# Three GpSimd subtractions and one more split weight pair at the start of the expert stage

## The chip, the cores and the metric

The kernel runs on one core of one Trainium2 chip. The metric is the time of one execution in device microseconds; before the change the median of three runs is 1587.92 us (1586.55 to 1590.53). Matrix products run on PE (TensorE), elementwise work on DVE (VectorE), ACT (ScalarE) and POOL (GpSimd), and SP issues most of the DMAs.

## The reference

One layer of an encoder on 1024 tokens of width 1024: an input projection, three mixers side by side (retention, S5, windowed attention), an output projection, a LayerNorm, then an expert-choice SwiGLU and a last LayerNorm. The change lies in the experts:

```python
def expert_choice_ffn(x, router_w, w_gate, w_up, w_down):
    cap = EC_FACTOR * seq // N_EXPERTS                       # 128 tokens for each of 16 experts
    aff = jax.nn.softmax(jnp.einsum('bld,de->ble', x, router_w), axis=-1)
    gates, idx = lax.top_k(jnp.swapaxes(aff, 1, 2), cap)
    xs = x[bidx, idx]
    hdn = jax.nn.silu(jnp.einsum('becd,edf->becf', xs, w_gate)) * jnp.einsum('becd,edf->becf', xs, w_up)
    out = jnp.einsum('becf,efd->becd', hdn, w_down) * gates[..., None]
    return jnp.zeros_like(x).at[bidx, idx].add(out)
```

All of it is in float32, with 2048 hidden columns for each expert.

## The kernel before, in words

**Pieces.** The weights of the 16 experts come as 384 pieces of 128 x 2048 float32 (1 MB each), numbered in the order of their use (`order`, built in `Experts.__init__`). A quarter of an expert takes four pieces for the gate and up products and, one quarter late, two pieces of the down product. So pieces 0 to 3 are the first quarter's gate and up, 4 to 7 the second's, 8 and 9 the first quarter's down, 10 to 13 the third's gate and up, 14 and 15 the second's down.

**Split or whole.** A split piece is brought to the form of two numbers: `high` (L2288) makes ACT round it to fp32r, `low` (L2297) makes DVE subtract that from the raw piece, and `mm3_piece` (L2228) does 12 matmuls of 512 columns: first four with the high parts of both sides, then four with the tokens' low parts, then four with the weights' low parts. Only the last four need the result of `low`. The pairs in `WHOLE` (pieces 0 and 1, 4 and 5, 10 and 11) are not split: `load_whole` (L2278) brings two pieces into one buffer, and `mm_whole` (L2236) does 4 matmuls in float32 on tokens that are float32 as well. They need neither ACT nor DVE.

**Order.** The order on each engine is written out by hand. After piece t, `quarter` issues `high` for piece t + 4 and `low` for piece t + 3. `low` of a piece also issues the load (L2271) of the piece that stands five places further in the list of split pieces, into the buffers of `wraw`, of which there are five; such a load waits until the buffer's last reader is done, and SP issues its DMAs strictly in order.

**The top-k beside it.** The first expert's tokens are known early (from a ranking of expert 0 alone). The top-k of all experts (`top_k`) runs while the first expert's pieces are worked on, one step after each piece, on DVE and PE: eight rounds of maxima (L2111, L2114), then a bitonic merge (`bitonic`, L1866 and L1867: maximum and minimum of two halves of one SBUF tile), with the copies L2124 and the maxima L2126 between its three parts, at last the reversed copy `rev` (L2130). Two transposes on PE (L2133, L2134) stand behind it, then `mm` on DVE (L2136, L2137), a transpose (L2140), `tau` and `taus` on DVE (L2142, L2144), a transpose (L2147), the flags `g` (L2150) and the counting matmuls (L2155 to L2161), from which come the slots, the one-hot tiles (L2174) and the gather of the second expert's tokens by GpSimd (L2190).

Of the kernel before, what the change touches and what calls it, by code (L numbers as in the profile page):

```python
# [9 lines left out]
F32 = mybir.dt.float32  # L10
# [5 lines left out]
OP = mybir.AluOpType  # L16
# [28 lines left out]
def level(pool, n):  # L45

    pool.tile([P, n // 4], F32, name="level")
# [26 lines left out]
def constants(K, I):  # L74
    nc, cp = K.nc, K.consts
    K.ident = cp.tile([P, P], F32, name="ident")
    make_identity(nc, K.ident)
    K.mhalf = cp.tile([P, 4], F32, name="mhalf")
    nc.gpsimd.memset(K.mhalf, -0.5)
# [23 lines left out]
class Units:  # L103
# [9 lines left out]
    def high(self, i):  # L113
        u = self.K.hl[self.side].tile([P, 2, 1024], F32R, name="whl", tag="whl", bufs=2)
        self.K.nc.scalar.activation(u[:, 0, :], self.raw[:, i, :], AF.Copy)
        self.u[i] = u[:, 0, :], u[:, 1, :]

    def low(self, i):
        hi, lo = self.u[i]
        self.K.nc.vector.tensor_tensor(lo, self.raw[:, i, :], hi.bitcast(F32), OP.subtract)  # L120
# [1659 lines left out]
def attention_steps(K, F, zero, out, qs, mat, spaces):  # L1780
# [26 lines left out]
    for c in range(NT):  # L1807
# [21 lines left out]
        for j in range(2):  # L1829
            for low, kind in enumerate(("YS", "YT")):  # L1830
                at(c, kind, j, fn=lambda c=c, j=j, low=low: out_proj_split(K, c, j, low))
# [40 lines left out]
def top_k_consts(K):  # L1872

    nc, cp = K.nc, K.consts
    K.order01 = cp.tile([P, 2, P], BF16, name="order01")
    nc.gpsimd.memset(K.order01, 1.0)
    nc.gpsimd.affine_select(K.order01[:, 0, :], K.order01[:, 0, :], pattern=[[1, P]], base=-1, channel_multiplier=-1,
                            compare_op=OP.is_ge, fill=0.0)
    K.slots = cp.tile([P, P], F32, name="slots")
    nc.gpsimd.iota(K.slots, pattern=[[1, P]], base=-L, channel_multiplier=0, allow_small_or_imprecise_dtypes=True)  # L1880
    K.aff = cp.tile([P, NT, E], F32, name="aff")
    K.tok = cp.tile([P, NT, E, 5], BF16, name="tok")
    nc.gpsimd.iota(K.tok[:, :, :, 0], pattern=[[P, NT], [0, E]], base=0, channel_multiplier=0,
                   allow_small_or_imprecise_dtypes=True)
    nc.gpsimd.iota(K.tok[:, :, :, 1], pattern=[[0, NT], [0, E]], base=0, channel_multiplier=1,
                   allow_small_or_imprecise_dtypes=True)
    K.slot = cp.tile([P, NT, E], F32, name="slot")
# [351 lines left out]
class Experts:  # L2239
# [4 lines left out]


    RING = 6
    WHOLE = 0, 4, 10
    sort = None

    def __init__(self, K, I, O):  # L2250
        self.K, self.I, self.O = K, I, O
        self.order = []
        for q in range(4 * E + 1):
# [3 lines left out]
            if q:  # L2257
                e, f = divmod(q - 1, 4)
                self.order += [I["exp_w_down"][e, f, half] for half in range(2)]
        self.whole = [k + i for k in self.WHOLE for i in range(2)]  # L2260
        self.parted = [k for k in range(len(self.order)) if k not in self.whole]
# [18 lines left out]
    def high(self, k):  # L2280

        while self.highs <= min(k, len(self.order) - 1):
            k1, self.highs = self.highs, self.highs + 1
            if k1 in self.whole:
                continue
            pool, tag = (self.K.hy, "hy") if k1 in (6, 7) or k1 >= 12 and k1 % 6 not in (1, 3) else (self.K.hla, "whl")
            u = self.whl[k1] = pool.tile([P, 2, 2048], F32R, name="whl", tag=tag)
            self.K.nc.scalar.activation(u[:, 0, :], self.raw[k1].rearrange("p a b -> p (a b)"), AF.Copy)  # L2288

    def low(self, k):  # L2290

        while self.lows <= min(k, len(self.order) - 1):
            k1, self.lows = self.lows, self.lows + 1
            if k1 in self.whole:
                continue
            u, raw = self.whl[k1], self.raw.pop(k1).rearrange("p a b -> p (a b)")
            self.K.nc.vector.tensor_tensor(u[:, 1, :], raw, u[:, 0, :].bitcast(F32), OP.subtract)  # L2297
            i = self.parted.index(k1)
            if i > 1:
                self.load(i + 5)  # L2300
# [259 lines left out]
def build(tc, nc, I, O):  # L2560
    K = Ctx()
    K.tc, K.nc = tc, nc
    K.unit = 0

    def pool(name, side="left", **kw):
        cm = tc.tile_pool(name=name, bufs=kw.pop("bufs", 1), **({} if "space" in kw else {"side": side}), **kw)
        return cm, cm.__enter__()

    def close(*cms):
        for cm in cms:  # L2570
            cm.__exit__(None, None, None)

    _, dr = pool("scratch", space=DRAM)
    K.h_dram = [dr.tile([P, D], F32, name=f"h_d{t}") for t in range(NT)]
    K.y_dram = [dr.tile([P, 2, P], F32, name=f"y_d{t}") for t in range(NT)]
    K.q_dram = [[dr.tile([P, 4, 4, P], F32, name=f"q_d{h}_{k}") for k in range(2)] for h in range(2)]
    K.h1_dram = dr.tile([L, D], F32, name="h1_d")
    K.acc_dram = dr.tile([L, D], F32, name="acc_d")
    K.bx_dram = [[dr.tile([P, 8, 16], F32, name=f"bx_d{d}{g}") for g in range(2)] for d in range(2)]
    K.wo_dram = [[dr.tile([P, 8, 144], F32, name=f"wo_d{d}{g}") for g in range(2)] for d in range(2)]  # L2580
    K.s_dram = [[dr.tile([P, 8, P], F32, name=f"s_d{d}{g}") for g in range(2)] for d in range(2)]
    K.m_dram = [dr.tile([P, 8, P], F32, name=f"m_d{g}") for g in range(2)]
    K.kv_dram = [dr.tile([P, 2, 256], F32, name=f"kv_d{t}") for t in range(NT)]
    K.u_dram = dr.tile([P, 2, 8, P], F32, name="u_d")

    c_ps, K.pmm = pool("pmm", space=PSUM, bufs=2)
    c_pt, K.ptp = pool("ptp", space=PSUM, bufs=2)
    c_pa, K.pat = pool("pat", space=PSUM, bufs=2)
    c_po, K.po = pool("po", space=PSUM, bufs=1)
    c_sm, K.psm = pool("psm", space=PSUM, bufs=1)  # L2590

    c_con, K.consts = pool("consts")
    constants(K, I)
    K.gates = K.consts.tile([P, E], F32, name="gates")
    K.index = K.consts.tile([P, E], U32, name="index")
    top_k_consts(K)
    level(K.consts, 224)
    c_raw, K.raw = pool("raw", bufs=2)
    c_hy, K.hy = pool("hy", bufs=4)
    c_edge, edge = pool("edge", side="right")  # L2600
    level(edge, 224)
    hl = [pool(f"hl{i}", bufs=2, side="right") for i in range(2)]
    K.hl = [x[1] for x in hl]
    c_hl0, K.c_hl1 = (x[0] for x in hl)
    _, K.s5small = c_s5s = pool("s5small")
    c_s5s = c_s5s[0]
    K.c_ret, K.ret = pool("ret", side="right")
    K.S = K.ret.tile([P, NT, 256], F32, name="S")
    nc.gpsimd.memset(K.S[0:64, 0, :], 0.0)
    nc.gpsimd.memset(K.S[64:P, NT - 1, :], 0.0)  # L2610
    K.QT = K.ret.tile([P, 2, L], F32, name="QT")
    K.hT = [], []
    for half in range(2):
        for s in range(2):
            K.hT[s].append(K.hy.tile([P, KC, L // 2], F32R, name=f"hT{s}", tag="hy"))
    K.P, K.Y, K.at = {}, {}, {}
    T = mybir.EngineType
    hold = tc.manual_schedule(engines={T.PE, T.Activation, T.DVE, T.Pool, T.SP})
    hold.__enter__()
    K.mr, K.st, K.pr, K.ps, K.pt, K.pT, K.av, K.rpt, K.soft, K.ah, K.rank = ({} for _ in range(11))  # L2620
    X = K.X = Experts(K, I, O)
    K.next_raw = lambda k: (K.raw if k < 4 or (k - 4) % 5 > 2 else K.raw2).tile([P, 2, 1024], F32, name="wraw")
    K.psums, K.c_hl0 = (c_sm, c_po, c_pa, c_pt, c_ps), c_hl0
    c_ast, c_early, c_opy, c_op, c_tk, c_hla, c_xt = front(K, I, pool, close)
    close(c_tk, c_op, c_opy, c_early, c_ast, c_s5s)
    c_ex, K.ex = pool("ex")
    level(K.ex, 192)
    c_raw2, K.raw2 = pool("raw2", bufs=3)
    c_sel, K.sel = pool("sel")
    for half in range(2):  # L2630
        X.tokens(0, half, X.xF[:, half * 4:half * 4 + 4, :])
    for i in range(4, 6):
        X.load(i)
    expert_gather(K, 0, K.numbers)
    X.load(6)
    X.load_whole(10)
    X.sort = top_k(K)
    raw0 = []

    def sorted_out():  # L2640
        close(c_sel)
        raw0.append(pool("raw0", bufs=3))
        K.raw0 = raw0[0][1]
    K.sorted = sorted_out
    for q in range(4 * E + 1):
        X.quarter(q)
    last_rows(X, E - 1)
    assert not X.before and not X.after and not X.sort
    hold.__exit__(None, None, None)
    close(raw0[0][0], c_raw2, c_ex, c_hy, c_raw, c_con, c_xt, c_hla, c_edge, *K.psums)  # L2650
# [60 lines left out]
```

## Time and profile before

| what | value |
|---|---|
| median of three runs | 1587.92 us |
| the profiled execution | 1588.15 us |
| its span | 1586.4 us |
| granted TensorE clock | 0.993 |
| PE, DVE, ACT, POOL busy | 98%, 88%, 70%, 12% |
| subtractions L2297 on DVE | 378, 2285 ns each (median) |
| whole matmuls L2236 | 24, recorded as 48 |

In the profile's rows a group reads `line engine op out<-in shapes xcount`, with busy time and mean, and in brackets the idle time before it and what ended that. A float32 matmul of a whole piece is recorded as two entries, so a whole piece is `x8` and a split piece `x12`. Times in a timeline are microseconds from the start of the span. `SPq` rows are DMA issues.

### The profile page before, as it was taken

The numbers are of one execution on the slowest core, as the hardware profiler recorded it, in microseconds if no ns is written. First come the engines' busy times: TensorE is split into PE (matmuls) and PEld (weight loads), VectorE is DVE, ScalarE is ACT, GpSimd is POOL, SyncE is SP. The second block draws the span as 40 slices with busy tenths as digits, with TensorE's granted clock in tenths as the row PEclk, the third lists the DMA queues.
The fourth block names the chain that finished last, engine by engine and source line by source line (L and its number), as shares of the span: only waits on it lengthen the run. The fifth ranks groups of instructions, "written<-read, shape, count | busy, mean of one in ns | idle before, by whom it ended". The sixth has DMA issues, their size and how long they took to land.

```text
span 1586.4 us, 21018 instructions
## 1 busy us (share of the span) xinstructions
PE 1553.3 (98%) x7673; PEld 1277.0 (80%) x7673; DVE 1402.3 (88%) x1725; ACT 1118.2 (70%) x1281; POOL 191.9 (12%) x244
## 2 busy tenths in 40 slices
PE   7999999999989999999999999999999999999997
PEld 5887888788866788888888888888888888888886
DVE  7986974888887989999899998989999999999996
ACT  4645464877735677777777777777877878787783
POOL 4001211111110101010100101000201102020121
PEclk9999999999999999999999999999999999999999
DMA  5555569334258999999999999999999999999993
GB/s 183 207 153 128 148 195 283 103 95 147 102 195 347 357 387 403 383 389 395 371 385 384 372 385 377 398 410 418 405 413 414 405 414 415 410 413 415 408 421 145
DMA packets 101242, 506.78 MB, mean 319 GB/s; under 512 B 12817, under 2 KB 25873, under 8 KB 50450
## 3 DMA queue, kind: packets, MB, share of 16 engines
q1 hardware_dynamic: 84834, 474.50, 76.9%
q0 software_dynamic: 16304, 30.94, 6.9%
q8 instruction: 60, 0.98, 0.2%
q14 instruction: 44, 0.36, 0.1%
HBM read 461.36 MB, written 42.99 MB: 318 GB/s over the span
## 4 chain that ended last, share of the span: by engine, by line
PE 64%; DVE 14%; DMA 12%; issue 4%; ACT 4%; POOL 1%; SPq 0%; POOLq 0%; DVEq 0%; ACTq 0%
PE gu L2228 27%; PE y L2228 14%; DVE whl L2297 7%; DMA wraw<-in_exp_w_down 6%; PE mm L64 4%; PE mm L66 4%; PE mm L65 4%; DMA wraw<-in_exp_w_up 3%; PE tp L2211 2%; ACT whl L2288 1%; PE po L1458 1%; PE tp L1438 1%; PE at L1387 1%; DVE hT L56 1%; PE gu L2236 1%
## 5 line engine op out<-in xcount | busy, mean ns | idle before, releaser
L2297 DVE TENSOR_TENSOR whl<-wraw,whl 128x2048 fp32r<-128x2048 f32 x378 | 857.6, 2287 | 65.3 <-ACT whl L2288 62.9
L2288 ACT ACTIVATE whl<-wraw 128x2048 fp32r<-128x2048 f32 x378 | 724.2, 1919 | 244.7 <-PE gu L2228 69.1
L2228 PE MATMUL gu<-whl,xT 128*128 128x512 f32 x3000 | 712.3, 394 | 0.0
L2228 PEld LDWEIGHTS gu<-whl,xT 128*128 128x128 f32 x3000 | 555.4, 188 | 114.6 <-issue 1.0
L2228 PE MATMUL y<-whl,hT 128*128 128x512 f32 x1536 | 359.5, 389 | 0.0
L2228 PEld LDWEIGHTS y<-whl,hT 128*128 128x128 f32 x1536 | 288.0, 188 | 59.7
L2190 POOL DMA_INDIRECT xs<-h_d,index x15 | 29.9, 1992 | 456.5 <-PE y L2228 301.4
L64 PE MATMUL mm<-hT,whl 128*128 128x512 f32 x160 | 65.4, 409 | 0.0
L55 ACT ACTIVATE hT<-tp 128x512 fp32r<-128x512 f32 x80 | 46.0, 583 | 25.7 <-PE tp L163 14.3
L65 PE MATMUL mm<-hT,whl 128*128 128x512 f32 x160 | 62.5, 391 | 0.0
L66 PE MATMUL mm<-hT,whl 128*128 128x512 f32 x160 | 62.5, 391 | 0.0
L56 DVE TENSOR_TENSOR hT<-tp,hT 128x512 fp32r<-128x512 f32 x80 | 54.1, 683 | 4.2 <-ACT hT L55 4.1
L64 PE MATMUL mm<-WO,yh 128*128 128x512 f32 x128 | 53.4, 417 | 0.0
L66 PE MATMUL mm<-WO,yl 128*128 128x512 f32 x128 | 50.7, 396 | 0.0
L65 PE MATMUL mm<-WO,yh 128*128 128x512 f32 x128 | 50.5, 395 | 0.0
L64 PE MATMUL mm<-whl,hT 128*128 128x512 f32 (+1 forms) x128 | 47.2, 369 | 0.0
L2338 DVE TENSOR_TENSOR hid<-hid,gu 128x512 f32<-128x512 f32 x64 | 43.5, 680 | 3.8 <-PE gu L2228 3.8
L66 PE MATMUL mm<-whl,hT 128*128 128x512 f32 (+1 forms) x128 | 44.5, 347 | 1.5 <-DVE hT L56 1.5
L65 PE MATMUL mm<-whl,hT 128*128 128x512 f32 (+1 forms) x128 | 44.5, 348 | 0.1
L2332 ACT ACTIVATE hid<-gu 128x512 f32<-128x512 f32 x64 | 37.2, 581 | 8.4 <-PE gu L2236 8.4
L2211 PEld LDWEIGHTS tp<-ident,hid 128*128 128x128 f32 x256 | 31.3, 140 | 11.4 <-DVE hid L2338 3.7
L1398 DVE CUSTOM_DVE_ANT_0 S<-at,R,sink 128x384 f32<-128x384 f32 (+1 forms) x64 | 36.8, 577 | 3.9 <-PE at L1387 3.3
(429 smaller groups left out, 1778.0 us busy)
## 6 DMA issues: line engine op xcount, KB each, us to landing
wraw<-in_exp_w_up SPq DMA_DIRECT2D x128, 1024.0 KB, 8.1
wraw<-in_exp_w_down SPq DMA_DIRECT2D x128, 1024.0 KB, 8.6
wraw<-in_exp_w_gate SPq DMA_DIRECT2D x122, 1024.0 KB, 7.9
wraw<-in_w_in SPq DMA_DIRECT2D x8, 1024.0 KB, 7.5
whole<-in_exp_w_gate SPq DMA_DIRECT2D x6, 1024.0 KB, 10.2
x<-in_x SPq DMA_DIRECT2D x8, 512.0 KB, 4.5
h_d<-x SPq DMA_DIRECT2D x8, 512.0 KB, 3.2
q_d<-kst SPq DMA_DIRECT2D x32, 128.0 KB, 2.8
```

The lines of the kernel that those rows point to most:

```text
L55: nc.scalar.activation(hi, src, AF.Copy)
L56: eng.tensor_tensor(lo, src, hi.bitcast(F32), OP.subtract)
L64: nc.tensor.matmul(ps, a[0], b[0], start=start, stop=False)
L65: nc.tensor.matmul(ps, a[0], b[1], start=False, stop=False)
L66: nc.tensor.matmul(ps, a[1], b[0], start=False, stop=stop)
L1398: K.nc.vector.tensor_tensor_reduce(S[g][:, :W], K.at.pop((i, g))[:, :W], K.R[:, ro:ro + W], 2.0 ** -(h + 1), K.sink[:, h:h + 1], OP.add, O ...
L2211: K.nc.tensor.transpose(pt[:, c, :], src[:, (c0 + c) * P:(c0 + c + 1) * P], K.ident)
L2228: nc.tensor.matmul(ps, a[s][c], u[:, t, i * w:(i + 1) * w], start=first and id(ps) not in began, stop=last and left[id(ps)] == 0)
L2288: self.K.nc.scalar.activation(u[:, 0, :], self.raw[k1].rearrange("p a b -> p (a b)"), AF.Copy)
L2297: self.K.nc.vector.tensor_tensor(u[:, 1, :], raw, u[:, 0, :].bitcast(F32), OP.subtract)
L2332: nc.scalar.activation(self.h[q], self.pg[q][0], AF.Silu)
L2338: at(self.after, q, 3, lambda: nc.vector.tensor_tensor(self.h[q], self.h[q], self.pg[q][1], OP.mult))
```

## The change

`WHOLE` loses pieces 10 and 11. They are now split like the others: they come by `load` into `wraw`, ACT makes their high parts, and PE does 12 matmuls for each. `ASIDE` names pieces 7, 10 and 13: their subtraction is issued on GpSimd. Piece 11's subtraction is on DVE. The high parts and low parts of 10 and 11 lie in two buffers of the pool `hy`, where the whole pair had one. Pieces 7 and 13 leave DVE, piece 11 is new there.

```diff
-    WHOLE = 0, 4, 10
+    WHOLE = 0, 4
+    ASIDE = 7, 10, 13
...
-            pool, tag = (self.K.hy, "hy") if k1 in (6, 7) or k1 >= 12 and k1 % 6 not in (1, 3) else (self.K.hla, "whl")
+            pool, tag = (self.K.hy, "hy") if k1 in (6, 7, 10, 11) or k1 >= 12 and k1 % 6 not in (1, 3) else (self.K.hla, "whl")
...
-            self.K.nc.vector.tensor_tensor(u[:, 1, :], raw, u[:, 0, :].bitcast(F32), OP.subtract)
+            e = self.K.nc.gpsimd if k1 in self.ASIDE else self.K.nc.vector
+            e.tensor_tensor(u[:, 1, :], raw, u[:, 0, :].bitcast(F32), OP.subtract)
...
     X.load(6)
-    X.load_whole(10)
     X.sort = top_k(K)
```

In the changed kernel the lines stand one or two further down (L2288 becomes L2289, L2297 becomes L2299). On DVE, in the middle of the bitonic merge, before the change (`o64` and `m64` end the first part of the merge, `whl_5369` is piece 7, `hT1_5408` the low part of the first hidden quarter):

```order
L2124 COPY o64_5389<-b_5386 64x128
L2126 TENSOR_TENSOR m64_5391<-b_5386,o64_5389 64x128
L2297 TENSOR_TENSOR whl_5369<-wraw_5229,whl_5369 128x2048
L56 TENSOR_TENSOR hT1_5408<-tp_5398,hT0_5407 128x512
L1866 TENSOR_TENSOR b_5411<-m64_5391 64x64
```

and after it:

```order
L2124 COPY o64_5386<-b_5383 64x128
L2126 TENSOR_TENSOR m64_5388<-b_5383,o64_5386 64x128
L56 TENSOR_TENSOR hT1_5405<-tp_5395,hT0_5404 128x512
L1866 TENSOR_TENSOR b_5408<-m64_5388 64x64
L1867 TENSOR_TENSOR b_5408<-m64_5388 64x64
```

Piece 7's subtraction has left this place. At the end of the merge, on DVE before the change (`whl_5506` is piece 12, `whl_5526` piece 13, `whl_5552` piece 14):

```order
L2130 COPY rev_5504<-b_5501 32x128
L2136 COPY mm_5523<-tp_5520 128x16
L2137 TENSOR_TENSOR mm_5523<-mm_5523,tp_5520 128x16
L2297 TENSOR_TENSOR whl_5506<-wraw_5271,whl_5506 128x2048
L56 TENSOR_TENSOR hT1_5543<-tp_5533,hT0_5542 128x512
L2142 TENSOR_REDUCE tau_5548<-tp_5546 16x1
L2144 COPY taus_5550<-tau_5548 16x128
L2297 TENSOR_TENSOR whl_5526<-wraw_5372,whl_5526 128x2048
L2150 TENSOR_TENSOR g_5563<-aff_134,tp_5561 128x128 x2
```

and after it (`whl_5482` is piece 11, `whl_5510` piece 12, `whl_5567` piece 14):

```order
L2130 COPY rev_5508<-b_5505 32x128
L2299 TENSOR_TENSOR whl_5482<-wraw_5369,whl_5482 128x2048
L2136 COPY mm_5530<-tp_5527 128x16
L2137 TENSOR_TENSOR mm_5530<-mm_5530,tp_5527 128x16
L2299 TENSOR_TENSOR whl_5510<-wraw_5393,whl_5510 128x2048
L56 TENSOR_TENSOR hT1_5558<-tp_5540,hT0_5557 128x512
L2142 TENSOR_REDUCE tau_5563<-tp_5561 16x1
L2144 COPY taus_5565<-tau_5563 16x128
L2150 TENSOR_TENSOR g_5586<-aff_134,tp_5584 128x128 x2
```

Piece 11's subtraction stands between `rev` and `mm`, and piece 13's between `taus` and `g` is gone. On GpSimd, after the change (the rows ahead are the last steps of the top-k's preparation, `xs_5701` the gather of the second expert's tokens; `whl_5366`, `whl_5452` and `whl_5533` are pieces 7, 10 and 13):

```order
L1897 TENSOR_TENSOR rest1_5200<-rest0_5199,tok_135 128x16
L1895 CAST tok_135<-rest1_5200 128x16
L2299 TENSOR_TENSOR whl_5366<-wraw_5229,whl_5366 128x2048
L2299 TENSOR_TENSOR whl_5452<-wraw_5271,whl_5452 128x2048
L2299 TENSOR_TENSOR whl_5533<-wraw_5423,whl_5533 128x2048
L2190 DMA xs_5701<-h1_d_77,index_128 128x1024
```

The three stand in a row, between the preparation and the gather; before, nothing stood there.

## The prediction

> **What bounds the kernel now.** I read the page first, then the busy time by stages, then the chain that ended last around the first expert.
>
> ```profile
> span 1586.4 us, 21018 instructions
> core 0: us, PE busy (x) PEld busy (x) DVE busy (x) ACT busy (x) POOL busy (x), PEclk, DMA share, GB/s
> 481.00:500.60 19.60, 18.24 (x69) 12.11 (x68) 18.75 (x54) 10.43 (x7) 0.00 (x0) 1.00 0.99 409
> 500.60:523.00 22.40, 22.40 (x106) 15.35 (x107) 18.92 (x25) 13.36 (x10) 0.00 (x0) 1.00 0.69 240
> 560.00:1560.00 1000.00, 998.34 (x4642) 822.01 (x4641) 933.14 (x615) 776.18 (x570) 111.98 (x72) 1.00 1.00 399
> ```
>
> From 560 us on PE is busy 998 of 1000 us: what arrives late there stays late to the end. In the first expert (481 to 500.6) it is DVE that is full, 18.75 of 19.60 us, and PE is not. GpSimd does nothing. The chain says what DVE's work there decides:
>
> ```profile
> 483.27 2.20 DVE whl L2297
> 485.78 0.24 DVE b L1866
> 486.59 0.23 DVE o L2124
> 487.05 2.27 DVE whl L2297
> 489.33 0.60 DVE hT L56
> 491.36 2.20 DVE whl L2297
> 495.10 2.27 DVE whl L2297
> 500.20 0.21 DVE b L1866
> 500.60 0.24 PE tp L2133
> 500.85 0.25 PE tp L2134
> 501.10 0.59 PE tp L2211 x4
> 501.68 3.44 PE gu L2236 x8
> 505.23 3.44 PE gu L2236 x8
> 508.66 0.17 PE tp L2147
> ```
>
> From 483 to 500.6 us it runs through DVE alone: the subtractions of pieces 6, 7, 8 and 9 (four rows of L2297), and the steps of the merge between them, one after another. Then PE takes over: transposes, pieces 10 and 11, the next transpose. So each microsecond on DVE ahead of 500.6 counts, until PE no longer waits:
>
> ```profile
> 493.63 5.60 PE L2228 MATMUL y<-whl,hT 128*128 128x512 f32 x24
> 500.60 0.24 PE L2133 MATMUL tp<-ident,b 32*128 32x32 f32 x1 [1.36 <-DVE b L1867]
> 521.53 11.18 PE L2228 MATMUL gu<-whl,xT 128*128 128x512 f32 x48
> 500.58 0.21 DVE L2130 COPY rev<-b 32x128 f32<-32x128 f32 x1
> 501.34 0.17 DVE L2137 TENSOR_TENSOR mm<-mm,tp 128x16 f32<-128x16 f32 x1
> 505.72 2.27 DVE L2297 TENSOR_TENSOR whl<-wraw,whl 128x2048 fp32r<-128x2048 f32 x1
> ```
>
> PE waits 1.36 us for the merge; `rev` ends at 500.79.
>
> **The split pair on PE.** Four split pieces in a row take 11.18 us, a pair 5.59. The whole pair takes 3.44 + 3.44 = 6.88. Between the same transposes PE saves 6.88 - 5.59 = **1.29 us**, all on the path.
>
> **DVE's own work.** Piece 7's subtraction leaves the path ahead of `rev`: **-2.27 us**. Piece 13's (505.72, 2.27 us) stood beside PE's matmuls of piece 11: nothing. Piece 11's is new between `rev` and `mm`. Its cover is piece 10 on PE: that begins 501.68 - 500.79 = 0.9 us after `rev` and ends 0.9 + 2.8 = 3.7 us after it; 2.28 us of subtraction and some 0.4 us of `mm` are done by 2.7. Nothing, with 1.0 us to spare; a further hold of DVE there is paid beyond that 1.0.
>
> **GpSimd's three subtractions.** No row has one of this size. The nearest on the same engine:
>
> ```profile
> L257 POOL TENSOR_TENSOR rsmall<-rsmall 128x8 f32<-128x8 f32 x1 | 0.2, 205 | 0.1
> L261 POOL TENSOR_TENSOR w<-lg,col 128x4 f32<-128x4 f32 x2 | 0.4, 203 | 0.1
> L1897 POOL TENSOR_TENSOR rest<-aff,tok 128x16 f32<-128x16 f32 x8 | 1.8, 223 | 0.7
> ```
>
> From 4 to 16 columns it grows by 20 ns, 1.67 ns a column; from 8 to 16 by 18 ns, 2.25 a column. For 2048 columns that gives 0.2 + 3.4 = 3.6 us or 0.2 + 4.6 = 4.8 us. I take the middle, 4.2; the lower bound is DVE's 2.28 for the same shape.
>
> PE can wait that long. Piece 7's low part is needed for its last four matmuls only, and here is when ACT has the high parts:
>
> ```profile
> 481.32 1.91 ACT L2288 ACTIVATE whl<-wraw 128x2048 fp32r<-128x2048 f32 x1 [3.35 <-DMA wraw<-in_exp_w_up]
> 488.36 0.60 ACT L2332 ACTIVATE hid<-gu 128x512 f32<-128x512 f32 x1 [0.17 <-PE gu L2236]
> 488.86 1.91 ACT L2288 ACTIVATE whl<-wraw 128x2048 fp32r<-128x2048 f32 x1
> 496.60 1.92 ACT L2288 ACTIVATE whl<-wraw 128x2048 fp32r<-128x2048 f32 x1 [5.84 <-PE y L2228]
> ```
>
> Piece 7's ends at 483.23, so GpSimd can begin while DVE is on piece 6; piece 10's now stands at 488.86 and ends at 490.8. ACT's two new roundings fit into the 5.84 us in which it waited.
>
> What matters is whether the two engines can run side by side:
>
> ```profile
> 1255.28 4.49 DVE L2297 TENSOR_TENSOR whl<-wraw,whl 128x2048 fp32r<-128x2048 f32 x2
> 1258.33 1.48 POOL L2466 TENSOR_SCALAR fst<-fst 128x1 f32<-128x1 f32 x1 [4.49 <-ACT yl L2465]
> 446.86 2.30 DVE L2297 TENSOR_TENSOR whl<-wraw,whl 128x2048 fp32r<-128x2048 f32 x1
> 446.73 0.29 POOL L1897 TENSOR_TENSOR rest<-rest,tok 128x16 f32<-128x16 f32 x1
> 447.08 2.17 POOL L1895 CAST tok<-rest 128x16 bf16<-128x16 f32 x1
> L2297 DVE TENSOR_TENSOR whl<-wraw,whl x378: 2271/2285/2301, 446.9 to 1564.5; 128x2048 fp32r<-128x2048 f32 x189
> ```
>
> A one-column GpSimd step at 1258.33 takes 1.48 us and ends at 1259.81, with DVE's subtraction (1259.77). A 16-column cast that falls into a subtraction takes 2.17 us and ends at 449.25; the subtraction ended at 449.16. So GpSimd stands still while DVE subtracts two SBUF tiles. The other direction shows faintly: the one subtraction at whose start a GpSimd step was already running (446.73) is the longest of all 378, 2301 ns against 2285. I take it that whoever starts first holds the other for its whole run. The Trainium skill says so too ("SBUF — State Buffer", "Who interferes with whom"): DVE with two SBUF inputs and GpSimd reading SBUF exclude each other, and issue order decides; the trace agrees for DVE ahead of GpSimd and has no long case of the reverse. This rule speaks against the change.
>
> All merge steps L1866 and L1867 have two SBUF inputs, like the subtractions, and DVE works in order: one blocked step blocks the rest. Piece 7 on GpSimd starts behind piece 6's subtraction on DVE, at about 485.5, and holds the merge **4.2 us**, to 489.7. PE needs the result for the last third of piece 7, 2.8/3 = 0.9 us before it goes on to piece 8 at 493.63: 3 us to spare. Piece 10 is ready at 490.8, still inside the merge: **4.2 us** more. Now `rev` ends at 500.79 - 2.27 + 8.4 = 506.9.
>
> Piece 13's load waits for piece 8's subtraction on DVE (end of the third L2297 row, 493.56, now 493.56 - 2.27 + 8.4 = 499.7).
>
> ```profile
> DMA to landing us min/median/max: 4.7/7.8/18.6
> ```
>
> With DMA at 0.69 of its time here I take 4.7: landed at 504.4, rounded by ACT at 506.3. So GpSimd starts it at the last steps of the merge or at piece 11's subtraction right behind `rev`: **4.2 us** again, in the first case in full, in the second less the 1.0 to spare. With the median 7.8 it falls later, under PE's work on piece 11, and costs about 1.
>
> Nothing else is on the path. Piece 12's load waits on SP for GpSimd's piece 7, with 13 and 14 queued behind it; two pieces fewer lie ready in advance, but piece 12 lands by 489.7 + 4.7 = 494.4 and is needed past 508.66; without that cover PE would wait what is missing. The gather behind the three on GpSimd needs slots that depend on PE's work after piece 13: no delay of its own.
>
> Sum: -1.29 - 2.27 + 3 x 4.2 = **+9.0 us**. The 1.36 us that PE waits is at the same place, so none of the delay is absorbed. The profiled execution took 1588.15, of which 1586.4 is its span; 1597.2 there, and 0.2 less against the median of 1587.92: **1597 us**. With 3.6 and 4.8 for a hold it is +7.2 and +10.8: 1595 to 1599. The Trainium skill gives a size for GpSimd's step ("GPSIMD Engine Reference", 3.1): 4497 ns against DVE's 2293 for a tensor_tensor of 2048 float32; DVE's row agrees (2285), no row has the other, and by it the estimate would be +9.9.
>
> **The rivals.**
>
> *No hold in this direction.* GpSimd's reads slip in between DVE's. Then DVE is 2.27 us earlier at `rev`, PE's wait of 1.36 goes (what is late next is PE itself), and the split pair saves 1.29: -2.65, 1585.3 us. For it: no DVE step in the trace is seen waiting for microseconds on GpSimd. Against it: the clear wait in the other direction, and the 2301. It decides if the merge step behind piece 6's subtraction starts within 0.2 us.
>
> *Smaller holds.* If GpSimd is as fast as DVE, three holds of 2.28 give 6.84 - 3.56 = +3.3, 1591.2. If piece 13's falls under cover, 8.4 + 1 - 3.56 = +5.8, 1593.7.
>
> *More than the holds.* Holds of 4.8 and a PE wait on piece 13, which lands late (7.8 instead of 4.7, another 3.1): +13.9, 1601.8.
>
> **How the numbers follow.** Three full holds 0.50, smaller 0.20, none 0.22, more 0.08. A measurement of this kernel tells about 0.3%, 4.8 us, from no change: 1583.2 to 1592.7 is the same. Faster by more has no mechanism here, 0.03; the same takes the rest of no hold and half of the smaller ones, 0.29; slower 0.68. The range reaches from no hold (1585) to near the end of the last case (1601); the likeliest case has 1595 to 1599.
>
> **What would show it.** Right: three L2299 rows on POOL of about 4.2 us or more, the DVE step behind piece 6's subtraction starting some 4 us later, and PE's wait at L2133 grown from 1.36 to over 7 us, less what PE then waits at pieces 8 and 9. Pieces 10 and 11 take 5.6 us on PE. Wrong: DVE's steps keep their spacing beside GpSimd's rows, or PE's wait at L2133 is gone.

## The result, and the profile after

The changed kernel takes 1602.16 us (median of 6 runs, 1599.68 to 1605.08), the kernel before, run beside it, 1590.73 (6 runs, 1586.55 to 1591.47). The medians are 11.4 us apart. The ratio of the runs is 1.0078, 95% interval 1.0061 to 1.0095, which is 9.7 to 15.1 us: slower, by less than one per cent. The profiled execution took 1601.82 us, its span is 1600.1 us, the mean granted clock 0.990 (0.993 before).

The busy times of the changed kernel by stages; behind the stretch and its length stand PE, PEld, DVE, ACT and POOL, then the granted clock of TensorE, the DMA share and GB/s:

```profile
core 0: us, PE busy (x) PEld busy (x) DVE busy (x) ACT busy (x) POOL busy (x), PEclk, DMA share, GB/s
481.51:501.30 19.79, 15.60 (x55) 9.56 (x54) 19.25 (x33) 11.20 (x8) 9.19 (x2) 0.93 0.48 197
501.30:512.14 10.84, 5.66 (x17) 4.07 (x15) 10.53 (x22) 1.91 (x1) 4.49 (x1) 0.66 0.73 290
512.14:535.00 22.86, 22.80 (x116) 18.34 (x117) 19.08 (x24) 13.98 (x10) 1.00 (x1) 0.93 0.72 267
560.00:1560.00 1000.00, 996.75 (x4635) 820.29 (x4634) 932.84 (x619) 774.74 (x566) 114.80 (x72) 1.00 1.00 398
```

The steady part is as before: PE is busy 997 of 1000 us. The first two rows reach to the end of `rev`. Before, that took 19.8 us (481.00 to 500.79), and now it takes 30.6: DVE is "busy" nearly all of it, PE is not, and the clock, 1.00 before, is 0.93 and 0.66. GpSimd's rows in the changed kernel's timeline say what happened there:

```profile
482.25 4.61 POOL L2299 TENSOR_TENSOR whl<-wraw,whl 128x2048 fp32r<-128x2048 f32 x1 [21.03 <-ACT whl L2289]
491.36 4.58 POOL L2299 TENSOR_TENSOR whl<-wraw,whl 128x2048 fp32r<-128x2048 f32 x1 [4.49 <-ACT whl L2289]
507.57 4.49 POOL L2299 TENSOR_TENSOR whl<-wraw,whl 128x2048 fp32r<-128x2048 f32 x1 [11.63 <-ACT whl L2289]
```

and DVE's rows beside them, with piece 6's subtraction for comparison:

```profile
482.38 4.57 DVE L2120 TENSOR_TENSOR both<-half,half 128x64 f32<-128x64 f32 x1
488.05 2.28 DVE L2299 TENSOR_TENSOR whl<-wraw,whl 128x2048 fp32r<-128x2048 f32 x1
491.43 4.59 DVE L2124 COPY o<-b 64x128 f32<-64x128 f32 x1
507.59 4.55 DVE L2130 COPY rev<-b 32x128 f32<-32x128 f32 x1
```

Each GpSimd subtraction has one DVE step beside it that starts with it and ends with it. A waiting instruction is drawn as a long one here: the same three steps take 0.22, 0.22 and 0.21 us in the kernel before. So they were held for 4.35, 4.37 and 4.34, together 13.06 us. All three holds lie ahead of the end of `rev`, which comes at 512.14 in place of 500.79. PE in the changed kernel:

```profile
494.16 1.07 PE L2228 MATMUL y<-whl,hT 128*128 128x512 f32 x4
497.00 1.21 PE L2228 MATMUL y<-whl,hT 128*128 128x512 f32 x4 [1.77 <-DVE hT L56]
500.63 6.09 PE L2228 MATMUL y<-whl,hT 128*128 128x512 f32 x16 [2.42 <-DVE whl L2299]
507.61 0.24 PE L2133 MATMUL tp<-ident,b 32*128 32x32 f32 x1 [0.89 <-DVE b L1867]
512.20 0.31 PE L2134 MATMUL tp<-ident,rev 32*128 32x32 f32 x1 [4.34 <-DVE rev L2130]
512.43 1.11 PE L2211 MATMUL tp<-ident,hid 128*128 128x128 f32 x4
513.20 4.06 PE L2228 MATMUL gu<-whl,xT 128*128 128x512 f32 x12
517.13 2.98 PE L2228 MATMUL gu<-whl,xT 128*128 128x512 f32 x12
520.21 3.02 PE L2228 MATMUL gu<-whl,xT 128*128 128x512 f32 x12
```

Where PE waited 1.36 us before, it waits four times, 9.42 us in all, and every releaser is DVE; none is GpSimd. And something else is in these rows: piece 10 (513.20) takes 4.06 us where piece 11 with the same work takes 2.98, and the transposes of `hid` take 1.11 in place of 0.66. The granted clock of the changed kernel around it:

```profile
508.50:509.00 0.50, 0.00 (x0) 0.00 (x0) 0.50 (x1) 0.00 (x0) 0.50 (x1) 0.68 1.01 426
509.00:515.00 6.00, 2.80 (x9) 2.41 (x10) 5.97 (x5) 1.41 (x2) 3.06 (x1) 0.50 0.11 44
515.00:515.50 0.50, 0.50 (x3) 0.35 (x2) 0.50 (x1) 0.50 (x1) 0.00 (x0) 0.50 1.40 229
515.50:516.00 0.50, 0.50 (x4) 0.41 (x3) 0.50 (x1) 0.50 (x2) 0.00 (x0) 0.99 0.84 115
```

While PE stood still the clock fell to 0.50, and stayed there until 515.5, 3.3 us after PE had work again. From the transposes of `hid` to piece 12 go 520.21 - 512.43 = 7.78 us; with the whole pair it was 508.75 - 501.03 = 7.72. So the split pair saved nothing here.

### The profile page after: what moved, and what is told of

Its sections match the earlier page's. It is cut to its first block, busy times and chain, and to the rows that moved or that the text cites. A ratio compares the mean times of both kernels' runs of the same rounds, so it can differ in the third digit from the quotient of the medians.

```text
span 1600.1 us, 21040 instructions
## 1 busy us (share of the span) xinstructions
PE 1555.1 (97%) x7681; PEld 1279.8 (80%) x7681; DVE 1412.2 (88%) x1724; ACT 1122.3 (70%) x1283; POOL 206.8 (13%) x247
## 2 busy tenths in 40 slices
DMA packets 101242, 506.78 MB, mean 317 GB/s; under 512 B 12817, under 2 KB 25873, under 8 KB 50450
## 4 chain that ended last, share of the span: by engine, by line
PE 56%; DVE 18%; DMA 13%; issue 7%; ACT 5%; POOL 1%; SPq 0%; POOLq 0%; DVEq 0%; ACTq 0%
PE gu L2228 22%; PE y L2228 11%; DVE whl L2299 10%; DMA wraw<-in_exp_w_down 8%; PE mm L64 4%; PE mm L66 4%; PE mm L65 4%; DMA wraw<-in_exp_w_up 3%; ACT whl L2289 2%; PE tp L2211 1%; PE po L1458 1%; DVE hT L56 1%; PE tp L1438 1%; PE at L1387 1%; DMA wraw<-in_exp_w_gate 1%
## 5 line engine op out<-in xcount | busy, mean ns | idle before, releaser
L2299 DVE TENSOR_TENSOR whl<-wraw,whl 128x2048 fp32r<-128x2048 f32 x377 | 855.1, 2287 | 69.1 <-ACT whl L2289 67.3
L2289 ACT ACTIVATE whl<-wraw 128x2048 fp32r<-128x2048 f32 x380 | 728.3, 1919 | 249.9 <-DMA wraw<-in_exp_w_down 64.8
L2211 PE MATMUL tp<-ident,hid 128*128 128x128 f32 x256 | 39.3, 276 | 4.3 <-DVE hid L2340 4.2
L2211 PEld LDWEIGHTS tp<-ident,hid 128*128 128x128 f32 x256 | 31.3, 141 | 15.0 <-DVE hid L2340 7.7
```

The source lines that it names most:

```text
L2211: K.nc.tensor.transpose(pt[:, c, :], src[:, (c0 + c) * P:(c0 + c + 1) * P], K.ident)
L2299: e.tensor_tensor(u[:, 1, :], raw, u[:, 0, :].bitcast(F32), OP.subtract)
```

## The experiments

**The theories.** *Hold:* a GpSimd subtraction that reads SBUF stops DVE for its whole run, and three of them stand on the path. *Lateness:* the split pair itself is the trouble; two pieces fewer lie ready, and PE waits for loads, roundings and low parts. *Clock:* on top of the hold, PE's clock falls after the wait and takes back what the pair saves.

**How the runs are compared.** Traces of one kernel differ by some us in places that no edit touches, so besides the medians each trace is read at fixed points: the start of the four transposes of `hid` (L2211) in each quarter. At the first (484.29 us before) no edit has made PE wait yet; what a trace is late there, 0.1 to 4.5 us, is its front and is taken off. The column "ninth" is the delay against the kernel before at the ninth quarter (626.55 us before), less the front. e6_off_the_path and e11_off_the_path_2 have their edits behind that point, so their -0.48 and +0.27 show how far such a reading can be trusted: half a microsecond. "To piece 12" goes from the transposes of `hid` in front of piece 10 to the start of piece 12, with PE's waits in it. Each ratio is against the runs of the kernel before that stood beside that run (6, 13, 23 or 29, with medians from 1590.64 to 1591.08). The interval of a ratio covers whole executions; "ninth" and "to piece 12" come from one trace of each run.

| run | front | ninth | to piece 12 | median us | ratio to before, 95% |
|---|---|---|---|---|---|
| before | | | 7.72 | 1591.08 (29 runs) | |
| the change | 0.51 | +9.78 | 7.78 | 1602.16 | 1.0078, 1.0061 to 1.0095 |
| e1_dve_only | 1.96 | +2.70 | 8.70 | 1594.39 | 1.0019, 1.0002 to 1.0037 |
| e2_pool_only | 2.15 | +10.34 | 10.49 | 1601.52 | 1.0063, 1.0045 to 1.0081 |
| e3_dummy_reads | 3.13 | +12.56 | 9.20 | 1603.25 | 1.0081, 1.0064 to 1.0098 |
| e4_dummy_writes | 1.25 | +2.65 | 9.20 | 1590.57 (1 run) | |
| e5_pe_kept_busy | 0.12 | +9.15 | 7.11 | 1600.33 | 1.0063, 1.0042 to 1.0083 |
| e10_dve_only_pe_busy | 2.51 | +0.46 | 6.33 | 1591.88 | 1.0004, 0.9986 to 1.0021 |
| e6_off_the_path | 1.68 | -0.48 | | 1606.66 | 1.0099, 1.0077 to 1.0120 |
| e11_off_the_path_2 | 1.04 | +0.27 | | 1591.75 | 0.9996, 0.9974 to 1.0017 |
| e7_piece6_early | 3.51 | -3.14 | 7.73 | 1589.47 | 0.9989, 0.9976 to 1.0003 |
| e8_split_no_gpsimd | 4.54 | -0.03 | 7.54 | 1592.70 | 1.0011, 0.9996 to 1.0027 |
| e9_split_lows_spread | 1.04 | -0.33 | 6.33 | 1591.16 | 0.9986, 0.9966 to 1.0005 |

### Is it the hold?

**The split pair without GpSimd.**

```diff
-    ASIDE = 7, 10, 13
+    ASIDE = ()
```

> The changed kernel with the split third pair, but no subtraction on GpSimd: DVE makes the low parts of pieces 7, 10 and 13 too. Hold theory (GpSimd's subtraction stops DVE for its whole run, 3 x 4.35 us on the merge, which the changed kernel's trace shows as 4.57, 4.59 and 4.55 us steps): the holds go, piece 7's and piece 10's subtractions stand inside the merge (one more than before, +2.27), the split pair gives back 1.29, so about +1.0 us against the kernel before in the second quarter and after it, up to +2.5 if PE's clock falls after the wait for the merge as it did in the changed kernel; no DVE step of the merge longer than 0.3 us. Rival theory (the delay comes from the split pair itself: two pieces fewer lie ready in advance, more loads queue on SP, ACT has two more roundings): most of the +9.8 stays, with PE waiting for pieces 10 to 13.

PE in this run, from the transposes in front of piece 10 on:

```profile
504.63 0.31 PE L2133 MATMUL tp<-ident,b 32*128 32x32 f32 x1 [3.43 <-DVE b L1867]
...
505.12 1.12 PE L2211 MATMUL tp<-ident,hid 128*128 128x128 f32 x4
505.89 4.99 PE L2228 MATMUL gu<-whl,xT 128*128 128x512 f32 x12
```

`rev` ends at 504.83, which is 504.83 - 500.79 - 1.96 = 2.08 us late: the one subtraction more in the merge. PE waits for the merge and for no piece. So 7 of the 9.8 us go with GpSimd's subtractions, and lateness is refuted. The rest, +2.70, is above the +1.0 that I had worked out and a little above the +2.5 with a fallen clock: piece 10 takes 4.99 us, 2.0 more than at full clock, so the clock costs more here than in the changed kernel, though PE waited less.

**GpSimd without the split pair.** Pieces 10 and 11 whole again, pieces 7 and 13 on GpSimd:

```diff
-    WHOLE = 0, 4
-    ASIDE = 7, 10, 13
+    WHOLE = 0, 4, 10
+    ASIDE = 7, 13
...
     X.load(6)
+    X.load_whole(10)
```

> The kernel before with its three whole pairs, but the low parts of pieces 7 and 13 on GpSimd. Hold theory: piece 7's subtraction holds one step of the merge 4.35 us and leaves DVE (-2.27): +2.1. Piece 13's high part is ready at about 494 here, so its subtraction falls into the merge as well: +4.35, in all +6.4 at rev; PE's clock may fall after the longer wait for rev and add 1 to 1.5. Rival theory (loads and the split pair): about 0, as the loads and the pair are those of the kernel before. A second rival (GpSimd's result comes too late for PE): PE waits at the last matmuls of piece 7, and the merge keeps its spacing.

DVE's longest two steps of this run stand beside GpSimd's two (483.40 for 4.54 us, 500.76 for 4.86):

```profile
483.88 4.13 DVE L2119 TENSOR_TENSOR both<-half,half 128x64 f32<-128x64 f32 x1
...
501.76 3.93 DVE L1866 TENSOR_TENSOR b<-m 32x64 f32<-32x64 f32 x1
```

Both steps found GpSimd already running and waited for what was left of it. `rev` is 508.38 - 500.79 - 2.15 = 5.44 us late; expected were 6.4 with two full holds, and these two make 3.91 + 3.72 - 2.27 = 5.36. The rest comes behind it: 10.49 - 7.72 = 2.77 us from the clock (no wait of PE lies in that stretch, and the first whole piece takes 5.94 us in place of 3.60), and then PE waits 1.22 us for the gather (0.74 before) and 1.26 for `hid` (none before). Two subtractions on GpSimd alone make as large a loss as the whole change.

**Reads that nobody needs.** The kernel before, with GpSimd work added:

```diff
+            if k1 in (7, 12, 13):
+                for i in range(2):
+                    self.K.nc.gpsimd.tensor_tensor(self.K.junk, u[:, 0, i * D:i * D + D].bitcast(F32),
+                                                   self.xF.rearrange("p a b -> p (a b)"), OP.subtract)
...
+    K.junk = K.ex.tile([P, D], F32, name="junk", tag="xs", bufs=3)
```

> The kernel before, nothing left out, with GpSimd work added whose results nobody uses: behind the high parts of pieces 7, 12 and 13 two tensor_tensor of 128 x 1024 each, reading two SBUF tiles and writing a third, unused one. DVE keeps all its subtractions, PE and the loads are as before. Hold theory: three times some 4.35 us (two holds of 2.2 to 2.3 each) of which those ahead of rev count in full, those behind it less what PE's work there covers: +8 to +14 us; each DVE step that meets a GpSimd row is longer by about that row's time. Rival theories (lateness of GpSimd's results, the loads, the split pair): 0, as nobody waits for these results.

The second pair of added steps, at 494.04, falls into DVE's subtraction of piece 7. Its row on GpSimd, then DVE's:

```profile
494.04 6.76 POOL L2291 TENSOR_TENSOR junk<-whl,xF 128x1024 f32<-128x1024 f32 x2 [4.98 <-ACT whl L2288]
```

```profile
493.83 2.28 DVE L2301 TENSOR_TENSOR whl<-wraw,whl 128x2048 fp32r<-128x2048 f32 x1
496.03 0.67 DVE L56 TENSOR_TENSOR hT<-tp,hT 128x512 fp32r<-128x512 f32 x1
496.63 1.81 DVE L1866 TENSOR_TENSOR b<-m 64x64 f32<-64x64 f32 x1
498.37 0.21 DVE L1867 TENSOR_TENSOR b<-m 64x64 f32<-64x64 f32 x1
498.62 2.26 DVE L1866 TENSOR_TENSOR b<-b 64x64 f32<-64x64 f32 x1
```

Both directions stand in these rows. DVE was first at 493.83, so GpSimd waited 2.0 us (6.76 for two steps that take 4.80 elsewhere in this run). Then GpSimd was first, and DVE's merge steps waited, 1.81 and 2.26 us, one for each GpSimd step; `hT`, one of whose two inputs lies in PSUM, ran beside it in 0.67. Six merge steps are held for 11.5 us, and `rev` is 515.42 - 500.79 - 3.13 = 11.5 late. No load, no piece and no result had changed. So GpSimd steps that nobody waits for are enough to make DVE and the merge late: the hold is shown.

**Writes that nobody needs.** The same place, but GpSimd reads nothing (but for one column):

```diff
+            if k1 in (7, 12, 13):
+                self.K.nc.gpsimd.tensor_copy(self.K.junk[:, 0:1], u[:, 0, 0:1].bitcast(F32))
+                for i in range(5):
+                    self.K.nc.gpsimd.memset(self.K.junk, 0.0)
...
+    K.junk = K.ex.tile([P, D], F32, name="junk", tag="xs", bufs=3)
```

> The kernel before, nothing left out, with GpSimd work added that writes SBUF and reads nothing: behind the high parts of pieces 7, 12 and 13 a copy of one column and then five memsets of 128 x 1024 of an unused tile. If it is GpSimd's reads of SBUF that hold DVE, DVE's steps keep their lengths (subtractions 2.2 to 2.3 us, merge steps 0.2 to 0.3) and the first expert ends as before, within 0.5 us. If any long GpSimd instruction holds DVE, DVE's steps beside the memsets are longer by a memset's time and the expert ends several us later.

The memsets ran from 482.64, 492.39 and 500.19, five of 1.00 us each. DVE in this run:

```profile
484.44 2.28 DVE L2301 TENSOR_TENSOR whl<-wraw,whl 128x2048 fp32r<-128x2048 f32 x1
...
495.88 0.57 DVE L2124 COPY o<-b 32x128 f32<-32x128 f32 x1
...
502.17 1.06 DVE L2130 COPY rev<-b 32x128 f32<-32x128 f32 x1
```

Subtractions and merge steps keep their lengths beside 15 us of memsets. Two copies do not: `o` takes 0.57 in place of 0.21, `rev` 1.06. So it is not any GpSimd work that holds DVE: steps with two SBUF inputs waited beside GpSimd's subtractions, which read SBUF, and not beside its writes alone; copies from SBUF to SBUF waited beside its writes alone too. The Trainium skill ("SBUF — State Buffer", "Who interferes with whom") says both, the copies because they can enter a mode that takes both ports; these rows agree. My expectation of no more than 0.5 us was wrong: `rev` is 503.23 - 500.79 - 1.25 = 1.19 late, and the clock, which fell in this run, adds 9.20 - 7.72 = 1.48.

### Is it the clock?

**PE kept busy in the changed kernel.** 20 matmuls without a reader ahead of L2133:

```diff
+    for i in range(20):
+        nc.tensor.matmul(pt.rearrange("p a b -> p (a b)"), K.X.xT[0][0][:, 0, :],
+                         K.X.xT[0][0][:, 0:4, :].rearrange("p a b -> p (a b)"), start=True, stop=True)
     nc.tensor.transpose(pt[:, 0, 0:32], top, K.ident[0:32, 0:32])
```

> The changed kernel, with 20 matmuls of 128 x 512 added on PE ahead of the transpose L2133, whose results nobody reads (some 4.7 us, into the tile that the transpose then overwrites), so that PE does not stand still while rev is held. Clock theory (part of the loss is that PE's granted clock falls to 0.50 after it has stood still, which made piece 10 take 4.06 us and the four transposes of hid 1.11): piece 10 takes 2.8 to 3.0 us and the transposes 0.6 to 0.7, from the end of rev to the start of piece 12 go 6.6 us in place of 8.07, so the first expert ends about 1.4 us sooner than in the changed kernel; the three holds of DVE stay 4.3 us each. Rival (piece 10 is slow for another cause, its loads or its late low part): 8.07 stays, or grows.

Piece 10 takes 2.98 us and the transposes 0.66, as the clock theory has it. As a sum the run decides less, since the third hold fell elsewhere:

```profile
506.99 0.21 DVE L2130 COPY rev<-b 32x128 f32<-32x128 f32 x1
507.16 2.29 DVE L2302 TENSOR_TENSOR whl<-wraw,whl 128x2048 fp32r<-128x2048 f32 x1
507.35 6.57 POOL L2302 TENSOR_TENSOR whl<-wraw,whl 128x2048 fp32r<-128x2048 f32 x1 [11.76 <-ACT whl L2292]
```

GpSimd's third subtraction came behind piece 11's on DVE, waited for it, and then held piece 12's (5.39 us). So `rev` was done at 507.2, only 507.20 - 500.79 - 0.12 = 6.29 us late, the added matmuls kept PE until 510.04, and then PE waited 0.74 for `taus`. Of the 7.11 us to piece 12, 6.37 are work.

**The same without GpSimd.** `ASIDE = ()` as in the first run, and 14 such matmuls, where PE waited 3.43 us:

> The changed kernel without GpSimd's subtractions (DVE makes all), and 14 matmuls of 128 x 512 whose results nobody reads ahead of PE's transpose L2133, 3.3 us, where PE waited 3.43 us. Clock theory: the waiting is the same, but the clock does not fall: piece 10 takes 2.98 us in place of 4.99 and the transposes of hid 0.66 in place of 1.12, from the end of rev to piece 12 some 6.6 us in place of 8.99, and all behind it is 2.3 us sooner than without the added matmuls: +0.4 us against the kernel before in place of +2.7. Rival: the 8.99 us have another cause, and stay.

PE in this run:

```profile
501.58 3.33 PE L2134 MATMUL tp<-xT 128*128 128x512 f32 x14
505.18 0.24 PE L2136 MATMUL tp<-ident,b 32*128 32x32 f32 x1 [0.27 <-DVE b L1867]
...
505.60 0.66 PE L2214 MATMUL tp<-ident,hid 128*128 128x128 f32 x4
506.01 2.98 PE L2231 MATMUL gu<-whl,xT 128*128 128x512 f32 x12
```

The merge ends as late as without the matmuls (`rev` at 505.37, 2.07 late), but the clock stays at 1.00, to piece 12 go 6.33 us in place of 8.70, and the ninth quarter is +0.46 in place of +2.70. So matmuls without any use bring the ninth quarter 2.2 us forward, and the clock's part is shown. The medians, 1594.39 and 1591.88, agree with that, but the intervals of the two ratios overlap, so as a gain in the whole kernel's time it is not shown. The 6.33 also show what the split pair is worth at full clock: 7.72 - 6.33 = 1.39 us.

### What does a hold cost elsewhere?

**Eight subtractions far behind the top-k.** The kernel before, with the change's two lines that issue the named subtractions on GpSimd, and

```diff
+    ASIDE = 100, 130, 160, 190, 220, 250, 280, 310
...
```

> The kernel before with its three whole pairs, but the low parts of eight pieces far behind the top-k, one in every five experts' quarters or so (100, 130, 160, 190, 220, 250, 280 and 310), on GpSimd. Hold theory with the path: eight GpSimd steps of 4.5 us, each holds a DVE step for about 4.3 us, but there PE has its low parts some pieces ahead, so nothing of it reaches PE: 0 within 0.5 us at each of them. Rival (a hold costs its 4.3 us less the 2.28 that DVE saves wherever it stands, because DVE is 93% busy there): 8 x 2.1 = +17 us.

Neither theory is right. The delay grows by 1.96 us at piece 100, by 0 at 130, by 1.68 at 160, by 0 at 190, by 1.58 at 220. At piece 100, DVE and PE:

```profile
753.40 5.69 DVE L2174 TENSOR_TENSOR hot<-slot,slots 128x512 bf16<-128x512 f32 x2
```

```profile
759.15 0.25 PE L2183 MATMUL tp<-tok,hot 128*128 128x5 bf16 x4 [1.80 <-DVE hot L2174]
```

Here the held step is the one-hot tile `hot` (1.28 us for two in the kernel before), and PE stands at L2183 for it. I had counted only the low parts, which PE has pieces ahead, and not the other steps in DVE's row. At 130 and 190 it met subtractions, and cost nothing. The total, 1606.66 - 1591.08 = 15.6 us, is near the rival's 17, but not by its rule of 2.1 us each: of the first five two are free, and behind the thirty-ninth quarter the delay grows by 14.2 us, more than the last three would give. PE waits there eight times for `hid`, 12.9 us in all (1.3 us in the kernel before). How much of that is each piece's is not clear, since that part of the span varies by itself (below).

**Six at places without such a step.** The same with six other pieces:

```diff
+    ASIDE = 58, 82, 106, 130, 154, 178
...
```

> As the run with eight subtractions on GpSimd far behind the top-k, but six (pieces 58, 82, 106, 130, 154 and 178), all at places where the DVE steps next to come are subtractions and not the one-hot tiles (hot) or the product hid that PE waits for. Hold theory with the path: each holds a subtraction on DVE by some 2 to 4.4 us, PE has those results ahead, and nothing is lost: 0 within 0.3 us at each. Rival (each costs what DVE loses, wherever it stands): about 1.7 us each, +10 us in all.

DVE beside GpSimd's fourth (840.51 for 4.86 us):

```profile
842.90 6.83 DVE L2299 TENSOR_TENSOR whl<-wraw,whl 128x2048 fp32r<-128x2048 f32 x2 [3.05 <-ACT whl L2289]
```

Two subtractions take 6.83 in place of 4.5 us, PE does not wait, and the delay grows by 0.2 us about the first of the six and by 0.00 at the other five. The ratio is 0.9996 (0.9974 to 1.0017). A hold costs only what the reader of the held step cannot wait.

### Is there a better version?

**Piece 6's subtraction one piece sooner,** in DVE's idle 3.82 us ahead of the merge, nothing else:

```diff
-            self.low(lead)
+            self.low(lead + (self.taken == 2))
```

> The kernel before, with nothing on GpSimd, but the subtraction of piece 6 issued one piece sooner, where DVE waits 3.82 us for PE's products. If the merge on DVE is what PE waits for at L2133: rev ends 2.27 us sooner, PE's wait of 1.36 us there goes, and the second quarter and all behind it is 1.36 us sooner; PE is then the bound. Rival (PE's wait there is made by something else, or piece 6's high part is late): 0.

PE no longer waits at L2133, and behind the merge the delay is -1.63, near the -1.36 expected. It goes on to -2.46 at the fourth quarter, where PE's wait of 0.74 for the second expert's tokens is gone too, and -3.14 at the ninth. As a time, 0.9989 (0.9976 to 1.0003) is no difference that these runs can tell.

**The split pair, nothing on GpSimd, DVE's order changed.** `ASIDE = ()`, `WHOLE = 0, 4`, and

```diff
-            self.low(lead)
+            self.low(lead + {2: 1, 7: -1, 8: -1}.get(self.taken, 0))
```

> The third pair split as in the changed kernel, no subtraction on GpSimd; on DVE the subtraction of piece 6 one piece sooner (in DVE's idle time), piece 10's behind rev in place of inside the merge, piece 11's behind mm. Hold theory: no hold is left, rev ends 2.27 us sooner than before, PE's wait of 1.36 us and with it any fall of the clock goes, and the split pair gives its 1.29 us: -2.65 us against the kernel before, behind piece 11 on PE. Rival (the split pair itself costs: its loads, its roundings or its low parts come late): PE waits at pieces 10 to 13, and the gain is 0 or less.

`rev` is 2.16 us sooner and PE's wait at L2133 is gone. But the -2.65 expected did not last: the ninth quarter is at -0.03. PE's waits behind the merge name what took it:

```profile
PE tp L2211 <- DMA xs<-h_d,index: 1.7, 1, 1.7
PE tp L2147 <- DVE taus L2144: 1.2, 1, 1.2
```

Two subtractions stood ahead of `taus`, and the gather of the second expert's tokens, which hangs on the top-k, came late.

**The same with the subtractions spread.**

```diff
-            self.low(lead + {2: 1, 7: -1, 8: -1}.get(self.taken, 0))
+            self.low(lead + {2: 1, 7: -1, 8: -1, 9: -1}.get(self.taken, 0))
```

> The kernel with the split third pair and nothing on GpSimd, piece 6's subtraction one piece sooner, piece 10's behind rev, and now piece 11's behind mm and piece 12's and 13's behind taus, so that no second subtraction stands ahead of taus, for which PE waited 1.16 us in the last version. If the split pair's saving on PE is real and only DVE's order spent it: PE's wait at L2147 goes, and from the end of the fifth down piece to piece 12 PE needs 6.6 to 6.7 us against 7.96 from rev in the kernel before; the second quarter and what follows is 2.6 us sooner than in the kernel before, counted from the start of the merge. Rival (the gather of the second expert's tokens is the next bound): PE's wait for it at 533 us grows from 0.74 us by about what was saved, and at the second expert only 1.4 us are left.

The wait at L2147 is gone, and piece 12 starts 508.75 + 1.04 - 506.77 = 3.02 us sooner. Then PE waits:

```profile
533.06 0.63 PE L2211 MATMUL tp<-ident,xs 128*128 128x128 f32 x4 [1.61 <-DMA xs<-h_d,index]
574.67 0.66 PE L2211 MATMUL tp<-ident,hid 128*128 128x128 f32 x4 [1.05 <-DVE hid L2340]
```

The rival was right: 0.87 us more for the gather, then 1.05 for `hid`, and some 0.5 for `g`; of 3.0 us 0.3 are left. The pair's 1.39 us is real on PE, but of the 3.0 us the second expert's tokens come only 1.4 sooner (533.44 + 1.04 - 533.06), and the waits behind them take the rest. No version measurably beats the kernel before.

## Why the prediction was right or wrong

The forecast was slower, by three full holds, and that is what happened. The time, 1597, is 5.2 us short of 1602.16, and the range, to 1601, did not hold it. Point by point:

- **Three holds, 12.6.** Right in kind and number, 13.06 measured. GpSimd's step takes 4.49 to 4.61 us, between my middle (4.2) and the upper end (4.8). As its length, the 4497 ns of the Trainium skill ("GPSIMD Engine Reference", 3.1), which the prediction gave beside it, was the better value. The holds, 4.34 to 4.37 us, are a little shorter than the steps.
- **Where they fall.** I put the first behind piece 6's subtraction, at 485.5; piece 7 was rounded sooner and GpSimd started at 482.25, before it. It made no difference, as both are in the merge. Piece 13's was to be rounded by 506.3; it was at 507.5, with the front 0.5 later, and its subtraction caught `rev` in full, as the sum had taken it. That was luck: GpSimd started at 507.57 and `rev` at 507.59. In the run with PE kept busy, GpSimd started at 507.35, when `rev` had ended at 507.20, and `rev` was only 6.29 us late in place of 10.84. How often the changed kernel has the third hold in full is not known, since only one of its executions was traced.
- **DVE's own work, -2.27.** Right: `rev` is 512.14 - 500.79 - 0.51 = 10.84 us late, and 13.06 - 2.27 = 10.79.
- **Lateness.** Right: no PE row waits for GpSimd, and the first run without GpSimd keeps none of the delay that the pair's loads could make.
- **The split pair, -1.29.** This is the step of the mechanism that failed: between the transposes and piece 12 the pair gave +0.06 (7.78 against 7.72). "Pieces 10 and 11 take 5.6 us on PE" and the saving "all on the path" took PE's full clock for granted, while the same sum left PE standing for over 7 us. The clock fell, and took 7.78 - 6.33 = 1.45 us: shown by the two runs with PE kept busy, the one without GpSimd above all. The rows of before could not give the size, since there the clock is 1.00 throughout, but the long wait that the sum itself made should have raised the question.
- **Not in the sum:** PE's wait of 0.74 for the gather is gone, since PE comes later (-0.87 at that point), and in the quarters behind it another 0.29 goes, part of it a wait of 0.26 for `hot`.

Up to the ninth quarter that makes 9.78 against the 9.0 forecast: +0.46 for the holds, +1.4 for the clock, -1.2 for the waits that went. From there to the thirty-ninth quarter the delay does not change by more than 0.01. The other 4.4 us of the miss lie outside these terms: 2.8 are the level of the kernel before, the base of the sum (1587.92 for its first three runs, 1590.73 for six), and 1.6 are what the difference of the medians, 11.4, has above 9.78. The base is thus the term that was off by most. As 1602.16 is 1.2 us above the range, it would have lain inside without the clock's 1.4 us, and also without the base's 2.8. In the trace the delay grows by 3.3 us behind the thirty-ninth quarter, where PE waits for `hid` on DVE four times in the last experts (4.2 us); but over the same stretch the ten experiments without an edit there move by -1.5 to +5.6 us. Why those waits come and go was not tried. The range left no room for this scatter of the kernel's own time, which three runs did not show.

The rivals: *no hold* and *smaller holds* are refuted. *More than the holds* (1601.8) has the right time by another way: piece 13 did not land late, PE's clock and the level made it.

## What to carry to other kernels

GpSimd helps as a second elementwise engine only while DVE has no step due that it would hold, here a step with two SBUF inputs or a copy within SBUF. Before moving a two-tile step there, find out which DVE step is due at that time and how long its reader can wait, since that, not the sum of busy times, is the price. Where a change makes PE wait for some microseconds, ask what the work behind the wait costs at half clock (here 1.4 to 2.8 us more). A saving on one engine is worth what the next wait leaves of it: here the gather and `hid` stood right behind the split pair's gain.

## What the runs showed of the hardware

**The clock moves in steps of 3.41 us.** From half-microsecond windows, the times at half clock are, in the changed kernel, 498.44 to 505.27 and 508.68 to 515.51 (6.83 us each); with the pair on DVE alone 503.36 to 510.19 (6.83); with GpSimd alone 504.05 to 514.29 (10.24); with added reads 501.67 to 508.49 and 515.32 to 518.73; with added writes 503.14 to 506.55 (3.41); with PE kept busy 500.86 to 504.27 (3.41). All are one, two or three times 3.41. The Trainium skill ("TensorE: Matmul & The Clock Gate", Part 1) tells of a free-running window of 3413 ns, and the traces agree to 0.02 us. It gives an idle window as the condition for half clock; here less was enough. Ahead of 498.44 PE was busy for 0.20 + 1.21 = 1.41 of 3.41 us (41%) and the clock fell; in the run with added reads it was busy 1.56 of the 3.41 us from 508.49 on (46%), and the clock stayed. But the busy share alone does not decide it, since the changed kernel's second fall came behind a window with half of it busy (a row of its windows, read as above):

```profile
505.27:508.68 3.41, 1.69 (x7) 0.97 (x6) 3.19 (x13) 1.91 (x1) 1.11 (x1) 1.00 1.03 432
```

Of these 1.69 us, 0.24 are the one small transpose L2133; whether such a step counts less is not known. The clock came back only behind a window that was busy almost throughout: stretches with 63% busy (503.36 to 506.78, DVE alone) and 79% (507.46 to 510.88, GpSimd alone) left it at half. So a wait's cost depends on how it lies in that grid, which would explain 1.45, 2.37 and 2.77 us behind waits of 4.34, 3.43 and 5.70. These shares come from modelled ends of matmuls, and few windows; the exact condition stays open.

**A copy from one SBUF tile is held too.** `o` (64x128) and `rev` (32x128) were held 4.4 and 4.3 us by GpSimd's subtraction, and for part of a 1.00 us memset by GpSimd's writes, beside which two-tile steps ran freely. The prediction had told of two-input steps alone.
